# Hybrid SSD and gated-MLP block: a later place for one broadcast load, four small products and the splits of the turned copies

## The chip, the cores and the metric

The kernel runs on one core of a Trainium2 chip. The metric is device microseconds of one execution, the median of the timed runs. Before the change that is 978.47 us, the median of three runs (978.17, 978.47 and 980.12).

## The reference

One layer works on 256 latent tokens and 256 context tokens of width 2048. Cut to what matters here:

```python
zx = hx @ w_in                      # hx: normalised, modulated latents; 2048 wide in, z, u, v, m wide out
vn = rmsnorm(v) ; sg = w_s @ vn + b_s
y_b = rmsnorm(u * sg * silu(z_mlp)) * g_mlp     # the MLP half
y_a = rmsnorm(y_ssd * silu(z_ssd)) * g_ssd      # the SSD half
out = rmsnorm(concat(y_a, y_b) @ w_out) * g_post
x   = x + gate * out                # gate = silu(c) @ w_ada[:, 4096:] + b_ada[4096:]
```

All inputs are float32. A product with float32 weights is made of three TensorE products: each operand is split into a rounded part (hi) and the rest (lo), and hi*hi, hi*lo and lo*hi are summed. So each weight costs a cast on ScalarE (hi) and a subtraction on VectorE (lo) before TensorE can use it.

## The kernel before

**Stages.** The first 425 us make the modulation and the first projections and run the SSD scan. Then come the *latents*: sixteen blocks of 512 output columns, in the order v (blocks 0 to 3), u (4 to 7), m (8 to 11) and z (12 to 15). A block is 96 matmuls of 128x512: 16 slices of the inner dimension, two halves of the tokens, three products each. After the blocks come two output projections (`oproj`) and the finish.

**The weights' stream.** Weights come in 1 MB pieces on the queue of SyncE into four buffers. Half a piece at a time, ScalarE makes `hi_w` (L87) and VectorE `lo_w` (L88), each into one of four buffers; a half is worth 12 matmuls. The code asks for the split of a half three halves ahead of its use.

**What follows a block.** After a block of kind m or z, `lat_z` (L1123) takes its two PSUM tiles: ScalarE makes silu (`sz`), VectorE multiplies it into `vt` or `y`, ScalarE squares it for the norm. Then `lat_t` (L1057) turns the 512 columns: VectorE transposes 32x32 squares into a tile `T`, and sixteen DMAs of 32 KB, issued by GpSimd, put the squares in their places in a tile `Z` (the small transfers). Then `lat_split` (L1070), four times for a group: ScalarE makes the hi part of a turned slice times its norm weight (`hhi` or `yah`), VectorE the lo part (`hlo` or `yal`). They are operands of the output projections, a hundred microseconds and more later.

**The gate.** In blocks 1 to 8 VectorE sums the sixteen parts of the gate (`gate_tile`, L1011; its scratch tile is `junk`). `gate_bcast` (L1016), three units after block 9, makes from it a tile `G` of gate times g_post, the *output scale*, which only the finish uses. It loads g_post into G, broadcast to 128 partitions (1 MB written, queue of GpSimd), brings the gate into rows (a matmul `psgt`, then `gh`, `gl`), and then four times (`expand`, `spread`) VectorE makes a tile `gd`, TensorE spreads it over the partitions (`pg`, one matmul of 48x512) and VectorE multiplies the result into a quarter of G. There is one buffer for `gd`.

**What sets the order.** `later(dt, fn)` puts a function in a queue at a due time, in units that are meant as microseconds; `pump(1.3)` after every sixth matmul runs what is due. A block is 16 pumps, or 20.8 units. This gives the order in which the program is written down. From block 1 on, that order is not the one that runs: a planner goes through the program with its own costs of the instructions, and gives each engine in turn, among the instructions whose inputs and buffers are ready at that moment of its own clock, the one that stands first in the program. Within an engine, the chip then keeps the order so found, and an instruction that has to wait holds back all behind it.

Of the kernel before, what the change touches and what calls it, by code (L numbers as in the profile page):

```python
# [15 lines left out]
P = 128  # L16
# [31 lines left out]
def tile_hybrid_ssd_mlp(  # L48
# [19 lines left out]
    nc = tc.nc  # L68
    ORDER = _tile_order()

    def mkpool(**kw):
        return tc.tile_pool(reuse_waits="tile", **kw)
# [72 lines left out]
    def bc(ap, axis, n):  # L145
        u = ap.unsqueeze(axis)
        shp = list(u.shape)
        shp[axis] = n
        return u.to_broadcast(shp)
# [22 lines left out]
    def spt(shape, name):  # L172
        return sps.tile(shape, F32, tag="s", name=name)
# [390 lines left out]
    def half(u):  # L564
        if pos[1]:
            split_to(u + 4)
        else:
            later(0.1, lambda: split_hi(u + 3))
            later(1.4, lambda: split_lo(u + 3))
        return halves.pop(u)  # L570
# [6 lines left out]
    def later(dt, fn):  # L577
        queue.append((now[0] + dt, seq[0], fn))
        seq[0] += 1

    def pump(dt=0.0, flush=False):
        now[0] += dt
        while True:
            due = [q for q in queue if flush or q[0] <= now[0]]
            if not due:
                return
            q = min(due)
            queue.remove(q)
            q[2]()
# [409 lines left out]
    def open_lat():  # L999
        cvs.close()  # L1000
        L_["big"] = ctx.enter_context(mkpool(name="big", bufs=2, side="right"))
        L_["lt2"] = lt.enter_context(mkpool(name="lt2", bufs=2))
        gsp = gs.enter_context(mkpool(name="gsp", bufs=1))
        L_["vt"] = L_["big"].tile([P, 2, D], F32, tag="b16", name="vt")
        L_["cb2"] = gsp.tile([P, D], F32, name="cb2")
        L_["junk2"] = gsp.tile([P, D], BF16, name="junk2")
        nc.gpsimd.dma_start(L_["cb2"], crow.partition_broadcast(P))
        nc.scalar.activation(L_["cb2"], L_["cb2"], AF.Silu)


    def gate_tile(j):  # L1011
        raw = load_raw(wada[2 * KT + j], f"gate{j}")
        nc.vector.scalar_tensor_tensor(L_["junk2"], raw, 1.0, L_["cb2"], op0=ALU.mult, op1=ALU.mult,  # L1013
                                       accum_out=gate[:, j : j + 1])

    def gate_bcast():  # L1016
        gs.close()
        gp = ctx.enter_context(mkpool(name="gp", bufs=1, side="right"))
        G = gp.tile([P, D], F32, name="G")
        L_["G"] = G  # L1020
        nc.gpsimd.dma_start(G, gpost.partition_broadcast(P))
        nc.vector.tensor_tensor(gate[:, 0:16], gate[:, 0:16], pc[:, C_BADA + 32 : C_BADA + 48], op=ALU.add)
        nc.vector.tensor_copy(gate[:, 32:48], gate[:, 0:16])


        gh = gp.tile([48, P], F32R, name="gh")
        gl = gp.tile([48, P], F32R, name="gl")
        g1 = gp.tile([48, P], F32R, name="g1")
        gd = gp.tile([48, 4, P], F32R, name="gd")
        gk = gp.tile([48, KT], F32, name="gk")  # L1030
        nc.scalar.copy(g1, ones[0:48])
        nc.vector.tensor_tensor(gk, ident[0:48, 0:16], ident[0:48, 32:48], op=ALU.add)

        def rows():
            ps = spt([48, P], "psgt")
            nc.tensor.matmul(ps, lhsT=gate, rhs=ident, start=True, stop=True)
            nc.scalar.copy(gh, ps)
            nc.vector.tensor_tensor(gl, ps, gh.bitcast(F32), op=ALU.subtract)
            nc.vector.tensor_copy(gh[32:48], gl[32:48].bitcast(F32))

        def expand(j):
            nc.vector.tensor_tensor(gd, bc(gh.bitcast(F32), 1, 4), bc(gk[:, 4 * j : 4 * j + 4], 2, P), op=ALU.mult)

        def spread(j):
            p = spt([P, 512], f"pg{j}")
            nc.tensor.matmul(p, lhsT=g1, rhs=gd, start=True, stop=True)
            gb = G[:, j * 512 : (j + 1) * 512]
            nc.vector.tensor_tensor(gb, p, gb, op=ALU.mult)
            if j < 3:
                expand(j + 1)  # L1050

        later(2, rows)
        later(4, lambda: expand(0))
        for j in range(4):
            later(7 + 3 * j, lambda j=j: spread(j))

    def lat_t(kind, j4):  # L1057
        src = L_["vt"] if kind == 2 else y
# [11 lines left out]
    def lat_split(kind, j):  # L1070
        src = L_["Z"][:, :, j % 4]
        if kind == 2:
            gcol, hi, lo = C_GMLP, hhi[j][:, 0:256], hlo[j][:, 0:256]
        else:
            gcol, hi, lo = C_GSSD, L_["yah"][:, j, :], L_["yal"][:, j, :]
        hi, lo = (t.rearrange("p (t c) -> p t c", t=2) for t in (hi, lo))
        gc = pc[:, gcol + j : gcol + j + 1]
        nc.scalar.mul(hi, src, gc)
        nc.vector.scalar_tensor_tensor(lo, src, gc, hi.bitcast(F32), op0=ALU.mult, op1=ALU.subtract)
# [10 lines left out]
    def lat_vn(j4):  # L1090
        cols = slice(j4 * 512, (j4 + 1) * 512)
        gw = L_["lt2"].tile([P, 1024], F32, tag="gw", name=f"gw{j4}")
        gvb, ws = gw[:, 0:512], gw[:, 512:1024].rearrange("p (g q) -> p g q", g=4)
        nc.gpsimd.dma_start(gvb, gv[:, cols].partition_broadcast(P))
        nc.gpsimd.dma_start(ws, wsp[:, 4 * j4 : 4 * j4 + 4, :])
        for tk in range(2):
            vb = L_["vt"][:, tk, cols]
            nc.vector.scalar_tensor_tensor(vb, vb, rr[:, 0, tk : tk + 1], gvb, op0=ALU.mult, op1=ALU.mult)
        L_["ws"] = ws

    def lat_sg(j4):
        ws = L_["ws"]
        L_["sg"] = []
        for tk in range(2):
            p = spt([P, 512], f"psg{j4}{tk}")
            for gi in range(4):
                g = 4 * j4 + gi
                nc.tensor.matmul(p[:, gi * P : (gi + 1) * P], lhsT=ws[:, gi, :],
                                 rhs=L_["vt"][:, tk, g * P : (g + 1) * P], start=True, stop=True)
            L_["sg"].append(p)  # L1110
# [29 lines left out]
    for blk in range(16):  # L1140
        kind, j4 = divmod(blk, 4)
        if blk == 0:

            pa = [acp.tile([P, 512], F32, tag="acc", name="pa00"), spt([P, 512], "pa01")]
        elif blk % 2 == 0:
            pa = [acp.tile([P, 512], F32, tag="acc", name=f"pa{blk}{tk}") for tk in range(2)]
        else:
            pa = [spt([P, 512], f"pa{blk}{tk}") for tk in range(2)]
        if kind == 1:
            later(3 if j4 == 0 else 0, lambda j4=j4: lat_vn(j4))  # L1150
            later(10, lambda j4=j4: lat_sg(j4))
        for u in range(8):
            whi, wlo = half(base + blk * 8 + u)
            for kk in range(2):
                k = 2 * u + kk
                w = slice(kk * 512, (kk + 1) * 512)
                for tk in range(2):
                    t = slice(256 + tk * P, 256 + (tk + 1) * P)
                    nc.tensor.matmul(pa[tk], lhsT=hhi[k][:, t], rhs=whi[:, w], start=k == 0, stop=False)  # L1159
                    nc.tensor.matmul(pa[tk], lhsT=hhi[k][:, t], rhs=wlo[:, w], start=False, stop=False)  # L1160
                    nc.tensor.matmul(pa[tk], lhsT=hlo[k][:, t], rhs=whi[:, w], start=False, stop=k == KT - 1)  # L1161
                pump(1.3)
            if blk == 0 and u == 7:
                pump(flush=True)
                man.close()
                pos[1] = max(halves) + 1
                open_lat()
            if 1 <= blk < 9 and u % 4 == 1:
                gate_tile((blk - 1) * 2 + u // 4)
        if kind == 0:  # L1170
            later(0, lambda j4=j4, pa=pa: lat_v(j4, pa))
        elif kind == 1:
            later(0, lambda j4=j4, pa=pa: lat_u(j4, pa))
        else:
            later(0, lambda kind=kind, j4=j4, pa=pa: lat_z(kind, j4, pa))
            later(1.5, lambda kind=kind, j4=j4: lat_t(kind, j4))
            for jj in range(4):
                later(17 + jj, lambda kind=kind, j=4 * j4 + jj: lat_split(kind, j))
        if blk == 9:
            later(3, gate_bcast)  # L1180

# [4 lines left out]
    G, yah, yal = L_["G"], L_["yah"], L_["yal"]  # L1186
# [197 lines left out]
```

## Time and profile before

| | |
|---|---|
| median of the timed runs | 978.47 us (978.17 to 980.12) |
| the profiled execution's own time | 981.04 us |
| its span in the profile | 979.3 us |
| granted TensorE clock, mean | 0.996 |
| TensorE busy | 968.3 us (99%) |
| VectorE, ScalarE, GpSimd busy | 665.1, 496.0, 186.6 us |
| first matmul of block 9, 10, 11, 12 | 636.64, 658.40, 687.75, 709.64 us |

The profiled execution took 981.04 us, 1.74 us more than the span of its instructions and 2.57 us more than the median. Times inside it are microseconds from the start of the span. PE is TensorE, DVE is VectorE, ACT is ScalarE, POOL is GpSimd and SP is SyncE. A matmul of 128x512 is shown with about 0.39 us, but its successor starts 0.227 us later: the busy time of PE overlaps with itself, and time lost on PE is read from the distance of the starts or from the waits.

### The profile page before, as it was taken

How to read it: one execution, taken by the hardware profiler on the slowest of the kernel's cores; microseconds unless marked ns; L12 is line 12 of the kernel's file. 1: busy time of each engine (PE TensorE's matmuls, PEld its weight loads, DVE VectorE, ACT ScalarE, POOL GpSimd, SP SyncE). 2: the span in 40 equal slices, each digit the busy share in tenths (PEclk: the TensorE clock that was granted, in tenths of full speed). 3: DMA queues.
4: the chain of work that ended last, by engine and by line, in shares of the span. 5: the costliest groups of instructions: out<-in, count | busy, mean ns of one | idle time of the engine just before them, and what ended most of it. 6: DMA issues, size and time to landing. Idle time of an engine off the chain costs nothing.

```text
span 979.3 us, 13757 instructions
## 1 busy us (share of the span) xinstructions
PE 968.3 (99%) x5242; PEld 781.8 (80%) x5242; DVE 665.1 (68%) x1075; ACT 496.0 (51%) x757; POOL 186.6 (19%) x290
## 2 busy tenths in 40 slices
PE   9999999999999999999999999999999999999997
PEld 4688888787887878787888888886888888888885
DVE  6888798778876665755766776666666665445636
ACT  4344458666565454645444443444566564345522
POOL 0000002541462122124000000043333451000000
PEclk9999999999999999999999999999999999999999
DMA  9999953332333423146787778785666666556722
GB/s 366 417 415 415 371 217 130 110 133 86 129 106 132 151 86 130 47 169 221 300 301 281 266 255 309 269 302 168 213 209 199 235 219 207 201 186 241 271 89 86
DMA packets 37090, 211.45 MB, mean 216 GB/s; under 512 B 6417, under 2 KB 6673, under 8 KB 14369
## 3 DMA queue, kind: packets, MB, share of 16 engines
q1 hardware_dynamic: 30240, 192.91, 53.2%
q0 software_dynamic: 6208, 16.85, 5.2%
q8 instruction: 41, 0.67, 0.3%
q10 hardware_dynamic: 576, 0.82, 0.2%
q14 instruction: 25, 0.20, 0.1%
HBM read 204.20 MB, written 2.16 MB: 211 GB/s over the span
## 4 chain that ended last, share of the span: by engine, by line
PE 78%; DMA 11%; DVE 6%; issue 3%; ACT 2%; POOL 0%; SPq 0%; DVEq 0%; ACTq 0%; POOLq 0%
PE psx L141 9%; PE psx L143 9%; PE psx L142 9%; PE pa L1159 7%; PE pa L1160 7%; PE pa L1161 7%; DMA gate<-in_wada_dram 5%; PE pm L1202 3%; PE pm L1201 3%; PE pm L1200 3%; DMA ada<-in_wada_dram 3%; DVE lo_w L88 3%; PE pq L1202 2%; PE pq L1201 2%; PE pq L1200 2%
## 5 line engine op out<-in xcount | busy, mean ns | idle before, releaser
L88 DVE TENSOR_TENSOR lo_w<-w,hi_w 128x1024 fp32r<-128x1024 f32 x173 | 209.7, 1221 | 127.9 <-ACT hi_w L87 127.9
L87 ACT CAST hi_w<-w 128x1024 fp32r<-128x1024 f32 x173 | 181.9, 1053 | 210.5 <-PE pa L1161 146.3
L1159 PE MATMUL pa<-hi_w,hhi 128*128 128x512 f32 x512 | 201.7, 394 | 0.0
L1160 PE MATMUL pa<-lo_w,hhi 128*128 128x512 f32 x512 | 200.2, 391 | 1.3 <-DVE lo_w L88 1.3
L1161 PE MATMUL pa<-hi_w,hlo 128*128 128x512 f32 x512 | 199.9, 390 | 0.0
L141 PE MATMUL psx<-hhi,hi_w 128*128 128x512 f32 (+1 forms) x400 | 153.4, 383 | 0.0
L143 PE MATMUL psx<-hhi,lo_w 128*128 128x512 f32 (+1 forms) x400 | 145.9, 365 | 0.0
L142 PE MATMUL psx<-hlo,hi_w 128*128 128x512 f32 (+1 forms) x400 | 145.7, 364 | 0.0
L1160 PEld LDWEIGHTS pa<-lo_w,hhi 128*128 128x128 f32 x512 | 96.4, 188 | 21.8 <-DVE lo_w L88 2.0
L1159 PEld LDWEIGHTS pa<-hi_w,hhi 128*128 128x128 f32 x512 | 96.5, 189 | 21.4 <-issue 1.6
L1161 PEld LDWEIGHTS pa<-hi_w,hlo 128*128 128x128 f32 x512 | 96.5, 189 | 20.3
L623 DVE SCALAR_TENSOR_TENSOR xbc<-psx,pc,xbc 128x248 f32<-128x248 f32 (+1 forms) x204 | 83.6, 471 | 34.5 <-ACT xbc L607 33.5
L548 DVE TENSOR_TENSOR lo_w<-w,hi_w 128x1024 fp32r<-128x1024 f32 x61 | 77.1, 1271 | 23.7 <-ACT hi_w L542 23.6
L1067 POOL DMA_DIRECT2D Z<-T x128 | 73.9, 584 | 97.4 <-DVE T L1062 28.8
L141 PEld LDWEIGHTS psx<-hhi,hi_w 128*128 128x128 f32 x400 | 75.5, 189 | 13.3 <-issue 2.9
L143 PEld LDWEIGHTS psx<-hhi,lo_w 128*128 128x128 f32 x400 | 75.4, 189 | 12.5
L142 PEld LDWEIGHTS psx<-hlo,hi_w 128*128 128x128 f32 x400 | 75.6, 189 | 12.2 <-issue 1.7
L542 ACT CAST hi_w<-w 128x1024 fp32r<-128x1024 f32 x61 | 63.5, 1044 | 26.0 <-PE psx L142 12.9
L1013 DVE SCALAR_TENSOR_TENSOR junk<-gate,cb 128x2048 bf16<-128x2048 f32 x16 | 36.7, 2291 | 27.9 <-DMA gate<-in_wada_dram 27.9
L1200 PE MATMUL pm<-hi_w,hhi 128*128 128x512 f32 x128 | 49.8, 389 | 0.0
L1201 PE MATMUL pm<-lo_w,hhi 128*128 128x512 f32 x128 | 49.8, 389 | 0.0
L1202 PE MATMUL pm<-hi_w,hlo 128*128 128x512 f32 x128 | 49.8, 389 | 0.0
(270 smaller groups left out, 1398.9 us busy)
## 6 DMA issues: line engine op xcount, KB each, us to landing
w<-in_wlat_dram SPq DMA_DIRECT2D x64, 1024.0 KB, 4.9
w<-in_wout_dram SPq DMA_DIRECT2D x32, 1024.0 KB, 4.8
w<-in_wxbc_dram SPq DMA_DIRECT2D x25, 1024.0 KB, 4.8
ada<-in_wada_dram SPq DMA_DIRECT2D x24, 1024.0 KB, 13.9
gate<-in_wada_dram SPq DMA_DIRECT2D x16, 1024.0 KB, 5.9
ada<-in_wada_dram SPq DMA_DIRECT2D x16, 512.0 KB, 12.3
R<-acs POOLq DMA_DIRECT2D x8, 1024.0 KB, 5.7
wst<-in_wst_dram SPq DMA_DIRECT2D x15, 480.0 KB, 12.9
```

Source lines behind the costliest of these rows:

```text
L87: nc.scalar.copy(hi, raw)
L88: nc.vector.tensor_tensor(lo, raw, hi.bitcast(F32), op=ALU.subtract)
L141: nc.tensor.matmul(ps, lhsT=whi, rhs=hhi[k][:, s], start=start, stop=False)
L142: nc.tensor.matmul(ps, lhsT=whi, rhs=hlo[k][:, s], start=False, stop=False)
L143: nc.tensor.matmul(ps, lhsT=wlo, rhs=hhi[k][:, s], start=False, stop=stop)
L623: nc.vector.scalar_tensor_tensor(ao, zi, cw[:, k : k + 1], ao, op0=ALU.mult, op1=ALU.add)
L1159: nc.tensor.matmul(pa[tk], lhsT=hhi[k][:, t], rhs=whi[:, w], start=k == 0, stop=False)
L1160: nc.tensor.matmul(pa[tk], lhsT=hhi[k][:, t], rhs=wlo[:, w], start=False, stop=False)
L1161: nc.tensor.matmul(pa[tk], lhsT=hlo[k][:, t], rhs=whi[:, w], start=False, stop=k == KT - 1)
L1200: nc.tensor.matmul(p, lhsT=yh[:, t], rhs=whi[:, w], start=j == 0, stop=False)
L1201: nc.tensor.matmul(p, lhsT=yh[:, t], rhs=wlo[:, w], start=False, stop=False)
L1202: nc.tensor.matmul(p, lhsT=yl[:, t], rhs=whi[:, w], start=False, stop=hf == 0 and j == 15)
```

## The change

Three due times change. The load of g_post into G leaves the start of `gate_bcast` and gets a due time six units behind it. The four `spread` steps go from 7, 10, 13, 16 to 17, 20, 23, 26 units behind it. The `lat_split` steps (eight groups of four) go from 17, 18, 19, 20 to 19, 20, 21, 22 units behind the end of their block. No instruction is added or taken away.

```diff
     def gate_bcast():
         ...
         L_["G"] = G
-        nc.gpsimd.dma_start(G, gpost.partition_broadcast(P))
         nc.vector.tensor_tensor(gate[:, 0:16], gate[:, 0:16], pc[:, C_BADA + 32 : C_BADA + 48], op=ALU.add)
         ...
         later(2, rows)
         later(4, lambda: expand(0))
+        later(6, lambda: nc.gpsimd.dma_start(G, gpost.partition_broadcast(P)))
         for j in range(4):
-            later(7 + 3 * j, lambda j=j: spread(j))
+            later(17 + 3 * j, lambda j=j: spread(j))
     ...
             for jj in range(4):
-                later(17 + jj, lambda kind=kind, j=4 * j4 + jj: lat_split(kind, j))
+                later(19 + jj, lambda kind=kind, j=4 * j4 + jj: lat_split(kind, j))
```

## Prediction, made before the changed kernel was run

> **What bounds the kernel now.** TensorE: it is busy for 99% of the span, so only time that TensorE loses can be won. I looked for where it loses any, first in the table of stretches, cut at the first matmuls of blocks 9 to 12 (columns: stretch, its length, busy time of each engine, granted clock, DMA share, GB/s).
>
> ```profile
> PE 968.3 (99%) x5242; PEld 781.8 (80%) x5242; DVE 665.1 (68%) x1075; ACT 496.0 (51%) x757; POOL 186.6 (19%) x290
> ```
> ```profile
> 636.64:658.40 21.76, 21.76 (x97) 18.02 (x96) 15.75 (x18) 10.55 (x15) 8.31 (x15) 1.00 0.85 296
> 658.40:687.75 29.35, 27.23 (x104) 19.39 (x102) 19.01 (x28) 14.02 (x24) 10.75 (x19) 0.94 0.61 199
> 709.64:731.40 21.76, 21.76 (x97) 18.02 (x96) 13.91 (x20) 13.56 (x21) 9.24 (x16) 1.00 0.65 218
> ```
>
> A clean block is 21.76 us, or 0.2267 us a matmul. Block 10 takes 29.35: 7.59 us more, and it is the block that holds the gate's products. The waits and the matmuls around them say where these go (timeline rows: start, duration, engine, line, tiles, in brackets the idle time before and what ended it).
>
> ```profile
> PE pa L1160 <- DVE lo_w L88: 1.3, 2, 0.8
> PE pg L1046 <- DVE gd L1042: 0.9, 1, 0.9
> ACT hhi L1078 <- DMA Z<-T: 7.5, 1, 7.5
> ```
> ```profile
> 671.98 0.50 PE L1160 MATMUL pa<-lo_w,hhi 128*128 128x512 f32 x1 [0.51 <-DVE lo_w L88]
> 673.02 0.40 PE L1161 MATMUL pa<-hi_w,hlo 128*128 128x512 f32 x1
> 674.27 0.49 PE L1046 MATMUL pg<-gd,g 48*128 48x512 f32 x1 [0.85 <-DVE gd L1042]
> 678.90 0.39 PE L1161 MATMUL pa<-hi_w,hlo 128*128 128x512 f32 x1
> 679.21 0.50 PE L1046 MATMUL pg<-gd,g 48*128 48x512 f32 x1
> 679.64 0.51 PE L1159 MATMUL pa<-hi_w,hhi 128*128 128x512 f32 x1
> ```
> ```profile
> 664.73:668.15 3.42, 2.96 (x12) 1.58 (x10) 2.66 (x5) 3.42 (x8) 0.00 (x0) 1.00 0.01 2
> 671.56:674.97 3.41, 2.14 (x7) 1.32 (x8) 3.34 (x6) 1.80 (x2) 3.41 (x7) 1.00 0.73 187
> 674.97:678.39 3.42, 3.42 (x9) 2.65 (x9) 2.72 (x4) 0.95 (x1) 2.76 (x5) 0.50 1.03 356
> ```
>
> The reader is to see four losses. Two waits for `lo_w`, 1.3 us together, and about 1.7 with the slow restart of the pipeline. One wait of 0.9 for the first `gd`. A stretch of 3.4 us at half clock, right behind a stretch of equal length in which PE was idle for 3.41-2.14 = 1.27 us, or 37%; it costs half of 3.41, 1.7 us. And the gate's own products: from 678.90 to the matmul after 679.64 would be two steps without `pg` (0.45 us); it is 0.31+0.43+0.34 = 1.08 (the last step is estimated like the first), so each `pg` costs 0.63, four 2.5 us.
>
> **Why lo_w was late** is in the rows of ACT, DVE and POOL.
>
> ```profile
> 655.88 1.05 ACT L87 CAST hi_w<-w 128x1024 fp32r<-128x1024 f32 x1 [1.67 <-PE pa L1161]
> 664.49 1.71 ACT L1078 ACTIVATE hhi<-Z,pc 128x256 fp32r<-128x256 f32 x4 [7.55 <-DMA Z<-T]
> 666.10 1.04 ACT L87 CAST hi_w<-w 128x1024 fp32r<-128x1024 f32 x1
> 670.74 2.32 DVE L88 TENSOR_TENSOR lo_w<-w,hi_w 128x1024 fp32r<-128x1024 f32 x2
> 673.53 0.68 DVE L1042 TENSOR_TENSOR gd<-gh,gk 48x512 fp32r<-48x512 f32 x1
> ```
> ```profile
> 454.11 0.54 POOL L1094 DMA_DIRECT2D gw<-in_gv_dram  x1
> L1098 DVE SCALAR_TENSOR_TENSOR vt<-vt,rr,gw x8: 746/750/752, 526.4 to 564.1; 128x512 f32<-128x512 f32 x8
> 640.76 0.54 POOL L1021 DMA_DIRECT2D G<-in_gpost_dram  x1 [82.36 <-DVE junk L1013]
> 647.10 4.65 POOL L1067 DMA_DIRECT2D Z<-T  x8 [5.81 <-DVE T L1062]
> 659.32 1.16 POOL L1067 DMA_DIRECT2D Z<-T  x2 [0.54 <-DMA Z<-T]
> ```
>
> The four `hhi` of the first group stand in ACT's order ahead of the next `hi_w`, and their small transfers land only at 664.4. ACT stands still for 7.55 us, and the weights' splits behind it come late. The load of G was issued at 640.76, ahead of the sixteen small transfers on the same queue.
>
> **The change, part by part.**
>
> *The load of G.* In the program it already stands behind the small transfers of two groups: `gate_bcast` is due three units after block 9, at about 662, and `lat_t` of block 9 at 1.5. It ran at 640.76 all the same, when the last `junk` freed its memory and POOL had nothing else. A load of the u blocks shows the same: it ran at 454.11, its data are used at 526.4. The planner takes what is ready; `T` of the first group was not (POOL waited 5.81 us for it). Six units later in the program make G no later ready, and nothing is ready in its stead. So I take its place and its time as unchanged, 0 us; cover is not needed.
>
> *The splits.* They too run by readiness: by the code the first two `hhi` of the group stand ahead of the `hi_w` of 655.88 (due at pump 14, that one before pump 15), and they ran behind it, all four at a stretch. Two units later the first two still stand ahead of the `hi_w` of 666.10 and take the same place; the last two may fall behind it. The second late `lo_w`, which ends at 673.06 less one lo of 1.2, that is about 671.9, has the same work ahead of it either way, and it alone sets when TensorE resumes (671.98). Bounds: 0 to -0.4 us; I take 0, since the later wait absorbs what the first gives.
>
> *The spreads.* TensorE is never idle in the plan, so there the place in the program does decide. The first `pg` moves from pump 9 of block 10 to pump 1 of block 11, the others to pumps 3, 5 and 7. What this removes: the wait of 0.9 for `gd`, which is ready since 674.2. With it the idle share of the stretch up to 674.97 falls from 37% to some 12%, as in the stretch at 664.73 (2.96 busy of 3.42, full clock behind it): the half-clock stretch goes, 1.7 us. The four products themselves cost 2.5 us here or there.
>
> *What is late next.* Without products and half clock, the 47 matmuls after 671.98 take 47 x 0.2267 + 0.1 = 10.8 us, so block 11 begins at 682.75 and not at 687.75. The second group's turned copies do not move with it.
>
> ```profile
> 679.00 2.88 POOL L1067 DMA_DIRECT2D Z<-T  x5 [1.27 <-DMA Z<-T]
> DMA to landing us min/median/max: 1.8/4.2/8.4
> 685.66 1.71 ACT L1078 ACTIVATE hhi<-Z,pc 128x256 fp32r<-128x256 f32 x4
> 687.27 0.58 ACT L1131 ACTIVATE sz<-pa 128x512 f32<-128x512 f32 x1
> 676.41 0.68 DVE L1048 TENSOR_TENSOR G<-pg,G 128x512 f32<-128x512 f32 x1
> 677.01 0.67 DVE L1042 TENSOR_TENSOR gd<-gh,gk 48x512 fp32r<-48x512 f32 x1
> 690.25 1.28 DVE L1133 TENSOR_TENSOR vt<-vt,sz 128x512 f32<-128x512 f32 x2
> ```
>
> The last of the sixteen is issued at 681.3 and needs at least 1.8: it lands at 683.1 or later. ACT wants it 687.75-685.66 = 2.1 us before block 11, now at 680.7, and waits 2.6 us. Behind it on ACT are `sz` and `hi_w`, and on DVE `hlo`, a `lo_w`, the two `vt`, and then the product into G and the second `gd`, for which the second `pg` waits on TensorE. From the first `hhi` to the end of the second `vt` it was 691.53-685.66 = 5.87 us, with one product into G (0.6) in between; then come G and `gd` (1.3): 683.3 + 5.3 + 1.3 = 689.9. TensorE comes to the second `pg` at 682.75 + 18 x 0.2267 + 0.63 = 687.5. That is a wait of 2.4 us at most, 2.0 if the planner puts `pg` two matmuls further back for it; if it puts G and `gd` ahead of `lo_w` and one `vt` (1.2 + 0.6), 0.4. Nothing in the trace shows this order, so I take the middle, 1.2. Cover for the weights is ample: the delayed `lo_w` is wanted only six pumps into block 11, at 692.
>
> *Sum.* -0.9 (wait for the first `gd`) + 1.2 (new wait for the second) = +0.3, and -1.7 where the half clock was. Against the profiled execution's own 981.04 this is 979.6. That execution is 2.57 us above the median, and of the three runs one, 980.12, stands 1.65 above the next: about the price of a half-clock stretch. I choose to read the median as a run without it, and add to it only the +0.3: **978.8 us**.
>
> By the Trainium skill (TensorE: Matmul & The Clock Gate, Part 1: The HAM clock gate) the activity window is 3413 ns long and free-running, so that the same program meets it in another phase each time. The stretch of half clock from 674.97 to 678.39 agrees in length, and it would make the -1.7 us a matter of the single run, as I chose. The same section has the clock fall after an idle window; in this trace it fell after one with 37% idle, so the measurement decides.
>
> **Rivals.**
>
> *The load of G does go behind the first small transfers.* For it speaks only that the program says so. DMA moves some 377 GB/s at best here, so 1 MB less ahead gives 2.8 us: ACT resumes at 661.7, both waits for `lo_w` (1.7) go as well as the 0.9. Block 11 then begins at 680.8, the second group lands 2.8 earlier too, and the new wait is 0 to 1.2: 978.5-2.6+0.6 = 976.5 us.
>
> ```profile
> 644.00:648.00 4.00, 4.00 (x20) 3.30 (x19) 4.00 (x6) 3.45 (x7) 0.90 (x2) 1.00 0.93 377
> ```
>
> *VectorE keeps up and the second `pg` waits for nothing.* For it: in block 10 three of four `pg` waited for nothing, with two pumps between them as after. Against: there no `vt` stood between. 978.5-0.9 = 977.6 us, down to 975.9 if the median had the half clock.
>
> *Slower: the second `pg` waits 2.0 to 2.4 us in one piece and the clock falls.* Place: 18 matmuls into block 11. From the point where PE's idle share of a 3.41 us stretch passes a limit between 13% and 37%, it costs 1.7 more: 978.5-0.9+2.2+1.7 = 981.5 us. Against: a wait of 2 us is often cut in two by the stretches' border. A sentence beside it: by the skill's idle window this would cost 979.8, since no window is wholly idle.
>
> **How the numbers follow.** The forecast (new wait between 0.4 and 2.0, 977.7 to 979.8) has 0.50, the load that moves 0.12, VectorE that keeps up 0.22, the fall of the clock 0.16. A measurement of this kernel tells about 0.2%, 2 us, from no change, so faster is under 976.5 and slower over 980.4. Faster: half of 0.12, a third of 0.22 and a little of the first, 0.19. Slower: most of 0.16 and a little of the first, 0.17. Same: 0.64. The range of 976.0 to 980.8 leaves out the lower end of two rivals and most of the slower one's upper part, some 2 in 10.
>
> **What would show it.** Right: the load of G still first on POOL, with the first small transfers behind it; ACT's wait of some 7.5 us for the first group as before, TensorE's two waits for `lo_w` too; no wait of the first `pg`, then in block 11; block 10 about 5 us shorter, block 11 longer by 2.5 us and by a wait for `gd`; ACT with a wait of about 2.6 us for the second group. Wrong: G's load issued behind 647, or ACT's wait under 5 us; then the planner does follow the due times. A time under 976 would mean that, over 981 that the new wait brought the clock down.

## The result and the profile after

The changed kernel takes **985.3 us** (median of 6 runs, 984.24 to 988.06) against 979.19 for the kernel before in the same batch (6 runs, 978.17 to 980.12). The ratio is 1.0066, with a 95% interval of 1.0051 to 1.0080: slower by 0.66%, 6.1 us. The prediction was 978.8 us, with a range of 976.0 to 980.8, so the time lies outside it, and on the side of the rival to which I gave a chance of 0.16.

The profiled execution of the changed kernel has a span of 986.3 us (its time is 988.06); before it was 979.3. Both profiled executions stand above their medians, by 1.9 us (981.04, before) and 2.8 us, so each is on the long side and the two are compared with each other. First the busy times by engine, from the page:

```profile
PE 969.6 (98%) x5242; PEld 782.2 (79%) x5242; DVE 664.3 (67%) x1075; ACT 495.4 (50%) x757; POOL 186.2 (19%) x290
```

TensorE does the same 5242 matmuls in nearly the same busy time (969.6 against 968.3 us), and the span is 7.0 us longer. So the loss is idle time of TensorE, and it is found with the table of stretches, cut at the first matmuls of blocks 9, 10, 11 and 12 (columns as in the prediction: stretch, length, busy time of PE, PEld, DVE, ACT, POOL, granted clock, DMA share, GB/s):

```profile
637.71:659.47 21.76, 21.76 (x98) 18.02 (x96) 15.65 (x18) 10.45 (x15) 8.00 (x14) 1.00 0.86 306
659.47:684.32 24.85, 23.19 (x99) 17.95 (x98) 14.60 (x19) 11.96 (x19) 11.01 (x20) 1.00 0.63 208
684.32:716.66 32.34, 26.82 (x101) 20.05 (x100) 18.25 (x24) 13.57 (x22) 9.20 (x16) 0.89 0.47 152
```

Of the kernel before, the one row of this table that the prediction did not show, block 11:

```profile
687.75:709.64 21.89, 21.89 (x97) 18.13 (x97) 13.67 (x17) 11.60 (x18) 9.22 (x16) 1.00 0.59 195
```

Block 10 became 4.50 us shorter (29.35 to 24.85), as was meant. Block 11 became 10.45 us longer (21.89 to 32.34): TensorE is busy for only 26.82 of it, and the granted clock is 0.89. The two together are 57.19 against 51.24, 5.95 us more. Of the 7.0 us of span, another 0.93 lie in block 8 (22.69 against 21.76), where this one execution shows a wait of 0.6 for a `lo_w`, ahead of all that the change touches.

The waits of TensorE and ACT on the changed kernel (engine, tile, line, who it waited for: total us, number, longest):

```profile
PE pg L1045 <- DVE gd L1041: 5.5, 1, 5.5
PE pa L1160 <- DVE lo_w L88: 1.7, 2, 1.1
PE pa L1159 <- ACT hi_w L87: 0.4, 1, 0.4
ACT hhi L1078 <- DMA Z<-T: 14.7, 2, 8.4
```

Of the 1.7 for `lo_w`, 0.6 is the wait in block 8; block 10 has 1.1 and the 0.4 for a `hi_w`. The wait of 0.9 us for the first `gd` is gone. In its place stands one wait of 5.5 us for a `gd`, and ACT waits twice for turned copies that arrive late, where before it waited once. The rows around the second wait, in order of time (timeline: start, duration, engine, line, operation, tiles; in brackets the idle time before it and what ended it):

```profile
642.47 0.54 POOL L1053 DMA_DIRECT2D G<-in_gpost_dram  x1 [84.00 <-DVE junk L1013]
648.81 4.64 POOL L1067 DMA_DIRECT2D Z<-T  x8 [5.81 <-PE pa L1161]
...
680.67 2.88 POOL L1067 DMA_DIRECT2D Z<-T  x5 [1.43 <-DMA Z<-T]
...
689.14 1.31 ACT L1078 ACTIVATE hhi<-Z,pc 128x256 fp32r<-128x256 f32 x3 [6.28 <-DMA Z<-T]
689.51 0.39 PE L1161 MATMUL pa<-hi_w,hlo 128*128 128x512 f32 x1
...
692.36 1.22 DVE L88 TENSOR_TENSOR lo_w<-w,hi_w 128x1024 fp32r<-128x1024 f32 x1
693.49 0.69 DVE L1133 TENSOR_TENSOR vt<-vt,sz 128x512 f32<-128x512 f32 x1
694.09 0.68 DVE L1047 TENSOR_TENSOR G<-pg,G 128x512 f32<-128x512 f32 x1
694.70 0.67 DVE L1041 TENSOR_TENSOR gd<-gh,gk 48x512 fp32r<-48x512 f32 x1
695.42 0.79 PE L1045 MATMUL pg<-gd,g 48*128 48x512 f32 x1 [5.52 <-DVE gd L1041]
696.14 0.79 PE L1159 MATMUL pa<-hi_w,hhi 128*128 128x512 f32 x1
```

Read backwards: the second `pg` starts at 695.42, when `gd` is done. Before `gd` on VectorE come the product into G, a `vt`, a `lo_w`, two `hlo`, another `vt` and the first two `hlo`; this chain began with the first `hhi` on ACT at 689.14, and that waited 6.28 us for the second group's small transfers, the last of which POOL had started before 683.55. The load of G still stands first on POOL, ahead of all small transfers.

The idle time cost the clock as well. The four stretches around the wait:

```profile
686.95:690.36 3.41, 2.95 (x13) 2.08 (x12) 0.68 (x2) 1.22 (x4) 0.00 (x0) 1.00 0.02 10
690.36:693.77 3.41, 0.00 (x0) 0.00 (x0) 3.02 (x6) 3.41 (x8) 0.00 (x0) 1.00 0.00 0
693.77:697.19 3.42, 1.77 (x4) 1.14 (x5) 3.42 (x6) 1.16 (x3) 0.04 (x1) 0.50 0.72 247
697.19:700.60 3.41, 3.41 (x10) 2.64 (x9) 2.92 (x4) 1.04 (x1) 3.41 (x7) 0.50 0.34 103
```

One stretch is wholly idle, and then the clock is at half for two. TensorE had work from 695.42 to 700.60 of it; half of these 5.18 us is 2.6 lost. So the 5.95 us of blocks 10 and 11 come together in this way: -0.9 (the wait for the first `gd`) -1.7 (the half clock of before) +5.5 (the new wait) +2.6 (the new half clock) +0.2 (waits for the first group's late weights, 1.1+0.4 in place of 1.3) = 5.7.

**Why the second group came so late** is in the weights' stream. The table of stretches again, two microseconds at a time (the two last columns are DMA), and the timeline of SP's queue with the load of one weight piece (1 MB), under the `lo_w` that it waited for. First the kernel after:

```profile
679.50:681.50 2.00, 2.00 (x10) 1.65 (x10) 1.23 (x1) 0.64 (x1) 0.83 (x2) 1.00 1.06 371
681.50:683.50 2.00, 2.00 (x11) 1.65 (x10) 0.61 (x1) 1.05 (x1) 2.00 (x4) 1.00 0.96 295
683.50:685.50 2.00, 2.00 (x11) 1.61 (x9) 0.61 (x1) 0.00 (x0) 0.05 (x1) 1.00 0.98 365
685.50:687.50 2.00, 2.00 (x9) 1.26 (x8) 0.00 (x0) 0.00 (x0) 0.00 (x0) 1.00 0.39 141
```
```profile
680.17 1.23 DVE L88 TENSOR_TENSOR lo_w<-w,hi_w 128x1024 fp32r<-128x1024 f32 x1 [1.00 <-ACT hi_w L87]
681.42 0.33 SPq L81 DMA_DIRECT2D w<-in_wlat_dram  x1
```

The same two views of the kernel before:

```profile
679.80:681.80 2.00, 2.00 (x9) 1.64 (x10) 1.23 (x2) 0.46 (x1) 2.00 (x4) 1.00 0.88 298
681.80:683.80 2.00, 2.00 (x8) 1.23 (x7) 1.38 (x2) 0.59 (x1) 0.09 (x1) 1.00 0.17 34
683.80:685.80 2.00, 2.00 (x10) 1.66 (x9) 1.04 (x3) 1.09 (x2) 0.00 (x0) 1.00 0.52 123
```
```profile
682.42 1.23 DVE L88 TENSOR_TENSOR lo_w<-w,hi_w 128x1024 fp32r<-128x1024 f32 x1 [1.39 <-ACT hi_w L87]
683.68 0.33 SPq L81 DMA_DIRECT2D w<-in_wlat_dram  x1
```

Before, the last small transfer of the second group was issued at 681.30 and its end came at 683.33: 2.0 us, in a DMA that was at 17%. The next piece of weights was asked for after that, at 683.68. In both kernels the load starts when a `lo_w` ends and frees a buffer (681.40, before 683.65), and the `hi_w` ahead of that `lo_w` had waited for TensorE (1.66 us, before 2.85). After, TensorE is ahead (block 11 begins 3.4 us earlier), has used up an earlier piece sooner, and so the next one is asked for at 681.42, in the middle of the last five small transfers. The last of them was issued at 682.97 and landed at 688.99: 6.0 us, with DMA at 96 to 98% until 685.5. From 684.1 to the landing the profile shows no work on VectorE or GpSimd, so neither of them holds the transfers up. The issue itself is also 1.7 us later than before. On VectorE the second group's `vt` and `T` stand behind the first group's `hlo`, and ACT came out of its wait for the first group at 666.38, before at 664.49. This delay is older than what the change moves: the last `junk` of the gate already starts at 639.62, before at 637.90.

In short: without the products in block 10 TensorE runs ahead, its pace brings a load of 1 MB among the second group's last small transfers, these land 4 us later, and ACT, VectorE and in the end TensorE stand still for them. The experiments test this.

### The profile page after: what moved, and what is told of

Its sections match the earlier page's. It is cut to its first block, busy times and chain, and to the rows that moved or that the text cites. A ratio compares the mean times of both kernels' runs of the same rounds, so it can differ in the third digit from the quotient of the medians.

```text
span 986.3 us, 13757 instructions
## 1 busy us (share of the span) xinstructions
PE 969.6 (98%) x5242; PEld 782.2 (79%) x5242; DVE 664.3 (67%) x1075; ACT 495.4 (50%) x757; POOL 186.2 (19%) x290
## 4 chain that ended last, share of the span: by engine, by line
PE 78%; DMA 11%; DVE 5%; issue 2%; ACT 2%; POOL 1%; SPq 0%; DVEq 0%; ACTq 0%; POOLq 0%
PE psx L141 9%; PE psx L143 9%; PE psx L142 9%; PE pa L1159 8%; PE pa L1160 8%; PE pa L1161 8%; DMA gate<-in_wada_dram 4%; PE pm L1201 3%; PE pm L1200 3%; PE pm L1202 3%; DMA ada<-in_wada_dram 3%; DMA Z<-T 2%; PE pq L1200 2%; PE pq L1201 2%; PE pq L1202 2%
```

## The experiments

The theories that the expectations name: the spreads alone make the loss (against: the later load or the later splits do, or all together); the wait is made by the weight piece that comes earlier; the spreads in block 11 cost nothing of themselves if the first group is in time (against: a product at a block's border is dear anywhere). The runs of the kernel before that each ratio goes by have medians of 978.74 to 978.80 (979.19 for the row "after"); a ratio need not be the quotient of two medians to the last digit. Summary first (stretches of each profiled execution; "ACT waits" are those for turned copies of the first and second group, where no other number is said):

| kernel | median us | ratio, 95% | block 10 | block 11 | ACT waits us | wait at `pg` |
|---|---|---|---|---|---|---|
| before | 979.19 | | 29.35 | 21.89 | 7.5 | 0.9 |
| after | 985.3 | 1.0066 (1.0051-1.0080) | 24.85 | 32.34 | 8.4, 6.3 | 5.5 |
| spreads alone | 985.27 | 1.0067 (1.0050-1.0084) | 22.71 | 31.37 | 11.6 in two | 4.9 |
| all but the spreads | 978.40 | 0.9991 (0.9980-1.0001) | 25.95 | 21.90 | 8.8 in two | 0.9 |
| spreads still later | 985.76 | 1.0067 (1.0047-1.0086) | 23.26 | 24.40 | 6.8, 5.1, five more | 0 |
| piece held too long | 988.87 | 1.0096 (1.0081-1.0112) | | | 11.9 in four | 1.7 |
| piece held | 980.78 | 1.0027 (1.0011-1.0043) | 24.62 | 28.44 | 8.1, 3.2 | 2.4 |
| after, G really behind | 985.11 | 1.0069 (1.0052-1.0086) | 22.34 | 30.03 | 5.6, 4.8 | 4.0 |
| before, G really behind | 977.24 | 0.9989 (0.9980-0.9999) | 24.82 | 21.89 | 3.7, 0.4 | 0 |
| G behind, spreads still later | 981.54 | 1.0027 (0.9994-1.0061) | 22.34 | 24.37 | 0, 0 | 0 |
| before, gate's parts earlier | 976.63 | 0.9973 (0.9962-0.9984) | 24.82 | 21.89 | 0 | 0 |
| after, gate's parts earlier | 976.73 | 0.9983 (0.9974-0.9993) | 22.33 | 24.38 | 0 | 0 |

### The spreads alone, and all but the spreads

In the kernel before one line is changed:

```diff
-            later(7 + 3 * j, lambda j=j: spread(j))
+            later(17 + 3 * j, lambda j=j: spread(j))
```

And in the kernel after the same line is put back:

```diff
-            later(17 + 3 * j, lambda j=j: spread(j))
+            later(7 + 3 * j, lambda j=j: spread(j))
```

> The kernel before with the four spreads alone moved (17, 20, 23, 26); load and splits as before. Theory A (the second spread runs into ScalarE's wait for the second group's turned copies, and that wait is long because a weight load now comes 2 us ahead of their last transfers): the splits add nothing, about 984 to 986 us, block 11 some 31 to 33 us long. Theory B (the splits behind the silu push the second half of T, and with it the small transfers, 1.5 us back, and that is what costs): about 979 to 981 us, the wait for the second gd under 3 us.

> The changed kernel with the four spreads back at 7, 10, 13, 16; load and splits as changed. Theory A: as the kernel before, 978 to 980.5 us, the first pg waiting about 0.9 us or a little more in block 10. Theory B: some of the loss stays, 982 us or more.

Measured 985.27 and 978.40 us. Stretches and wait of the kernel with the spreads alone:

```profile
658.47:681.18 22.71, 22.63 (x99) 18.02 (x98) 14.52 (x19) 12.04 (x19) 9.21 (x16) 1.00 0.61 207
681.18:712.55 31.37, 26.47 (x101) 19.81 (x100) 18.35 (x24) 13.56 (x22) 9.23 (x16) 0.89 0.49 158
```
```profile
PE pg L1046 <- DVE gd L1042: 4.9, 1, 4.9
```

The same wait and the same clock of 0.89 without the other two edits. And the other two edits without the spreads change nothing that can be told: the interval holds 1. The whole loss is the spreads, and the due times of the load and of the splits do nothing measurable, as the prediction had it for both.

### The spreads still later

```diff
-            later(17 + 3 * j, lambda j=j: spread(j))
+            later(27 + 3 * j, lambda j=j: spread(j))
```

> The changed kernel with the spreads ten units further back (27, 30, 33, 36): they fall on pumps 8 to 14 of block 11, when ScalarE has come out of its wait. Theory A: the wait for the second gd is gone, block 10 keeps its 24.9 us, block 11 takes about 25 to 27 us (four products and up to 2 us of wait for a late lo_w): 977 to 980 us. Rival C (block 11 bears no products in any place, since its VectorE is full): 983 us or more.

Measured 985.76 us, the time of rival C and not of theory A. The part about the place held, against rival C: blocks 10 and 11 take 47.66 us, 3.6 less than before, and no `pg` waits. The stretches of blocks 10, 11, 13 and 14, and ACT's waits:

```profile
658.40:681.66 23.26, 22.95 (x99) 17.95 (x98) 14.60 (x19) 11.96 (x19) 9.21 (x16) 1.00 0.60 205
681.66:706.06 24.40, 24.40 (x101) 18.44 (x100) 15.79 (x21) 10.75 (x17) 9.22 (x16) 1.00 0.66 222
727.82:751.74 23.92, 22.37 (x97) 17.91 (x96) 13.61 (x16) 13.19 (x19) 10.22 (x18) 1.00 0.58 197
751.74:775.26 23.52, 22.38 (x97) 17.86 (x96) 13.51 (x16) 11.80 (x18) 9.23 (x16) 1.00 0.61 203
```
```profile
ACT hhi L1078 <- DMA Z<-T: 24.7, 4, 6.8
ACT yah L1078 <- DMA Z<-T: 17.9, 3, 6.8
```

But now ACT waits for the turned copies of seven groups in a row, 5.1 to 6.9 us each. Blocks 13 and 14, clean in the kernel before, take 23.92 and 23.52; the first products of the output then wait 1.7 and 1.5 us more, and the clock falls at 806. While ACT waits, no `hi_w` is made, then several are made at once, and the pieces of weights are asked for in bunches: four between 713.3 and 724.9, then none until 738.2. Each bunch comes in the next group's small transfers. This is read from the order in one trace. So the late product into the second `pg` was not the only place where the loss could show: the late copies are what lasts, and the `pg` was only the first to meet them.

### One piece of weights held back

In the changed kernel, the piece that came at 681.42 is held back by a copy of one column from a turned tile into the piece's buffer, which the load then overwrites. The first version reads another group's tile than the second's:

```diff
-            raws[pos[0]] = load_raw(stream[pos[0]], f"w{pos[0]}")
+            if pos[0] == 73:
+                raws[73] = wp["raw"].tile([P, 2048], F32, tag="raw", name="w73")
+                nc.gpsimd.tensor_copy(raws[73][:, 0:1], L_["Z"][:, 0, 0, 0:1])
+                nc.sync.dma_start(raws[73], stream[73])
+            else:
+                raws[pos[0]] = load_raw(stream[pos[0]], f"w{pos[0]}")
```

> The changed kernel, with the one weight load that was issued at 681.4, ahead of the last five small transfers of the second group, held until those have landed (GpSimd copies one column of the turned tile into the load's buffer first, so the load waits for that copy; the column is then overwritten). Theory A: the last of the second group lands about 684 and not 689, ScalarE's second wait falls from 6.3 us to about 1 to 2, the wait for the second gd from 5.5 to 1 to 2, no half clock: 978.5 to 981 us. Theory B (the transfers are slow of themselves, having started 1.5 us later): landing at 687 or later, 984 us or more.

Measured 988.87 us. The tile that it read was the third group's by then, and the piece came at 699.51 instead of behind 682. The second group's copies did land 2.3 us after the last issue (681.91 after 679.62), and the wait at `pg` fell to 1.7; but TensorE then waited 4.7 us for a `hi_w` out of the held piece, block 12 took 24.94, and the clock was at half for 6.83 us from 711.26. So the time of this kernel says nothing on the question, but its second group does: no piece is asked for between 674.70 and 686.53, the last transfer lands 2.3 us after its issue, ACT waits 2.5 us and TensorE 1.7.

```profile
PE pg L1050 <- DVE gd L1046: 1.7, 1, 1.7
```

The second version plans the hold earlier, so that it reads the second group's tile, and sets the third group's small transfers behind it (the first line stands in `load_to`, the last around the transfers of `lat_t`):

```diff
+        n = 74 if n == 73 else n
...
+                L_["hold"] = nc.gpsimd.tensor_copy(raws[73][:, 0:1], L_["Z"][:, 0, 0, 0:1])
...
+                with (tc.issue_after(L_["hold"].ins) if (kind, j4) == (2, 2) else ExitStack()):
```

> The changed kernel with the weight piece that was loaded at 681.4 held until the second group's sixteen transfers have landed (GpSimd copies one column of Z into the piece's buffer first; the load overwrites it). In the run before this one the copy read the third group's tile, so the piece came 18 us late; now it reads the second's. Theory A (that load is what makes the last five transfers late): they land 2 to 3 us after the last issue and not 6, the wait for the second gd is 1 to 2.5 us and not 5.5, no half clock, 979 to 982 us. Theory B: the wait stays over 4 us, 984 us or more.

Measured 980.78 us, that is 4.5 us less than the changed kernel (3.8 by the two ratios, which go by runs of the kernel before in the same batch). Timeline rows, the wait, and the stretch of block 11:

```profile
684.01 0.33 SPq L535 DMA_DIRECT2D w<-in_wlat_dram  x1
685.87 1.31 ACT L1085 ACTIVATE hhi<-Z,pc 128x256 fp32r<-128x256 f32 x3 [3.18 <-DMA Z<-T]
```
```profile
PE pg L1051 <- DVE gd L1047: 2.4, 1, 2.4
```
```profile
684.16:712.60 28.44, 26.01 (x101) 19.48 (x100) 18.21 (x24) 13.57 (x22) 9.20 (x16) 0.94 0.57 186
```

The piece is asked for 2.6 us later (684.01 in place of 681.42). The last small transfer, issued at 682.46, then lands at 685.72, 3.3 us after and not 6.0. ACT's wait falls from 6.28 to 3.18, TensorE's from 5.5 to 2.4, and one half-clock stretch is left of two. The last issue moved by 0.5 us only. So most of the late landing is a collision with this one load of the weights' stream. What the profiled execution has left is a wait of 2.4 and one half-clock stretch, where the expectation had none; but it is the longest of the six (984.00), and three of them show a granted clock of 0.999, where it shows 0.997, so the half clock is not in every run. The hold also did less than was expected of it: the column is written by the first four of the sixteen transfers, the copy ran at 683.04, right behind the last issue, and the piece was asked for before the last transfer had landed. It moved the piece from ahead of the last issue to behind it.

The other kernels agree with this reading. Where the piece is asked for ahead of the last issue, the second group's last transfer lands late: 6.0 us after its issue in the changed kernel (piece 1.6 ahead), 5.8 with the spreads alone (1.2), 5.1 with the spreads still later (1.3), and 4.9 in the changed kernel with G behind, which follows (1.1). Where it is asked for behind the issue, the landing takes 2.0 (before), 2.2 (all but the spreads), 3.3 (piece held) and 3.7 (before, G behind). The lateness matters because the issue is late as well: in the four kernels named first it stands 1.3 to 1.7 us before the start of block 11, in the kernel before 6.4.

### The load of G truly behind the small transfers

The due time did not move the load. This edit does, by an order between the two (the last small transfer of the first group first):

```diff
+        with tc.issue_after(L_["zl", 2, 0].ins):
             nc.gpsimd.dma_start(G, gpost.partition_broadcast(P))
```

It was put into the changed kernel, into the kernel before, and into the changed kernel together with the spreads at 27.

> The changed kernel with the load of G in truth behind the first group's sixteen transfers on GpSimd's queue (an order edge from the last of them). If the load ahead of them costs them what 1 MB takes at 377 GB/s: the first group lands 2.8 us earlier, ScalarE's first wait falls from 8.4 to about 5.5 us, block 10 loses its waits for lo_w (23 us or less and not 24.9). The second group then still meets the spreads in block 11: 978 to 985 us in all, according to whether the second group lands by the end of block 10.

> The kernel before with nothing but the load of G behind the first group's transfers (order edge); spreads and splits at their old due times. Same reason as for the run with both: ScalarE's first wait 7.5 -> about 5, the waits for lo_w in block 10 gone, the first pg with a wait under 0.5: 975 to 977.5 us. If the load's place did not matter: 978 to 980.

> The changed kernel with the load of G behind the first group's transfers and the spreads at 27, 30, 33, 36. With the spreads at 27 alone ScalarE waited 5 to 7 us for the turned copies in each of seven groups, because the weight loads that had been held up by one such wait ran in a bunch into the next group's transfers. If the first wait starts that row, a shorter first wait (5 us) still starts it: 980 to 986 us. If it ends it: 974 to 977 us.

In the changed kernel: 985.11 us, no gain that can be told. G is issued at 658.46, behind all sixteen. Block 10 is clean, 22.34 us, without the waits for `lo_w`; the second group's copies are still late (ACT waits 4.75 us) and `pg` waits 4.0. In the kernel before: 977.24 us, at the edge of what can be told. Its block 10 has no wait of TensorE at all, and ACT waits little (stretch, then wait):

```profile
658.49:683.31 24.82, 24.82 (x104) 18.43 (x102) 18.92 (x28) 13.76 (x23) 9.21 (x16) 1.00 0.77 255
```
```profile
ACT hhi L1080 <- DMA Z<-T: 4.1, 2, 3.7
```

With the spreads at 27 as well, the ten runs fall into two clusters, five at 976.79 to 977.47 and five at 985.61 to 987.97; the median of 981.54 stands for neither. The profiled execution is of the lower cluster, and in it TensorE waits for nothing in these blocks; ACT waits once, 1.1 us, for the third group (the stretches of blocks 10 and 11):

```profile
658.74:681.08 22.34, 22.34 (x99) 18.11 (x98) 14.90 (x20) 12.75 (x21) 9.22 (x16) 1.00 0.75 259
681.08:705.45 24.37, 24.37 (x101) 18.45 (x100) 18.35 (x25) 12.86 (x20) 9.21 (x16) 1.00 0.63 215
```

The upper cluster is at the time of the kernel with seven late groups. Whether it is the same row of waits, started or not by how the first group lands, is not shown: no execution of that cluster has a profile. The granted clock of its runs is 0.994 to 0.997, in the lower cluster 0.998 to 0.999, and in the runs of the kernel with seven late groups 0.997 to 0.999, so the two need not be alike.

### The first group in time

If the first group's lateness starts all this, then an earlier start of the gate's work must help both kernels. The sixteen parts of the gate's weights (`gate_tile`), two a block in blocks 1 to 8, are put earlier, so that POOL is free and `junk` done long before the first turn:

```diff
+    GATES = {1: (1, 4, 6), 2: (1, 4, 6), 3: (1, 4, 6), 4: (1, 5), 5: (1, 5), 6: (1, 5), 7: (1,)}
+    gseq = list(range(16))
...
-            if 1 <= blk < 9 and u % 4 == 1:
-                gate_tile((blk - 1) * 2 + u // 4)
+            if u in GATES.get(blk, ()):
+                gate_tile(gseq.pop(0))
```

> The kernel before with the sixteen gate parts summed earlier (three a block in blocks 1 to 3, two in 4 to 6, the last in 7, where it was two a block in 1 to 8), everything else as before. The last gate part then holds back neither the first group's vt and T (4.2 us of wait on VectorE) nor the weight pieces in block 9, and G's memory is free before the first group's transfers. Theory A (the first group's lateness starts all of it): ScalarE's first wait falls from 7.5 us to under 2, block 10 takes 24.5 to 26 us and not 29.4, no later wait: 974 to 976.5 us, unless the extra megabytes in blocks 1 to 3 cost there. If the lateness comes from something else: 978 to 980.

> The changed kernel with the same earlier gate parts. Theory A: with the first group in time there is no late second group for the spreads in block 11 to run into: wait for the second gd under 1.5 us, 974.5 to 977.5 us, about as the kernel before with them, so the change's loss of 6 us is gone. Rival C (spreads at the border of two blocks are bad of themselves, since VectorE is full there): 5 to 6 us more than the kernel before with earlier gate parts, 980 to 984 us.

On the kernel before 976.63 us (10 runs, 976.49 to 977.17), a little above the 974 to 976.5 expected, and faster than the kernel before by 0.27% (0.16 to 0.38): this version beats both kernels. On the changed kernel 976.73 us. The blocks 10 and 11 of the first, then of the second:

```profile
658.55:683.37 24.82, 24.82 (x104) 18.43 (x102) 18.78 (x28) 13.03 (x21) 9.18 (x16) 1.00 0.62 211
683.37:705.26 21.89, 21.89 (x98) 18.12 (x97) 13.67 (x17) 11.60 (x18) 9.19 (x16) 1.00 0.59 195
```
```profile
660.59:682.92 22.33, 22.33 (x99) 18.11 (x98) 14.87 (x20) 12.74 (x21) 9.20 (x16) 1.00 0.64 213
682.92:707.30 24.38, 24.38 (x102) 18.44 (x100) 17.78 (x24) 12.14 (x19) 9.20 (x16) 1.00 0.58 195
```

Both make 46.71 us, TensorE busy throughout and at full clock. The products cost 2.5 us in the one block or in the other. With the first group in time, moving them does nothing, neither gain nor loss; so the border of blocks 10 and 11 is not a bad place of itself, and the change's loss needs the late first group. The collision itself is still there: in both, and in the profiled execution with G behind and the spreads later, a piece is asked for 1.1 to 1.4 us ahead of the second group's last issue, which lands 4.4 to 4.7 us later. But that issue now stands 6.9 to 9.6 us before block 11, and nothing waits for it. One limit: this edit moves G's load too (to 605.8), so it doesn't tell that load from the gate's parts; the kernel before with G alone behind, at 977.24, suggests that about half of the gain is G's 1 MB out of the first group's way (0.11% of 0.27%). In the changed kernel G alone behind did not help (985.11), so there it takes more than that.

## Why the prediction was wrong, point by point

- **The load of G: right.** It ran first on POOL at 642.47, ahead of the first small transfer at 648.81, and without the spreads the rest of the change measured 0.9991.
- **The splits: right in effect.** The last two of the first group did fall behind a `hi_w` (ACT had two `hhi` at 666.38 and two at 669.71). TensorE's waits for the first group's weights were 1.5 us and not 1.3, outside the 0 to -0.4 that I gave; but the kernel with all but the spreads has the same splits, shows none of these waits in block 10, and measures as before.
- **The spreads, in block 10: right.** The first `pg` went to block 11 (685.77) and waited for nothing, the wait of 0.9 and the half clock behind it are gone, and block 10 is 4.5 us shorter, where 5.0 was forecast.
- **What is late next: wrong, and this is the step that failed.** It names the right chain. From the first `hhi` to the end of the second `gd` it was 6.2 us (689.14 to 695.37), where I had 5.3+1.3 = 6.6; and TensorE came to the second `pg` after 21 matmuls of the block at 689.74, where I had 687.5. The term that failed is the landing of the second group: "it lands at 683.1 or later", and I went on with 683.3. It landed at 688.99. I had taken the shortest landing of all (1.8 us) on top of an issue time of the kernel before, with the words "or later" in the text and no upper end in the sum, although the same row had 4.2 as the median and 8.4 as the longest. Of the 5.7 us, 1.7 are the later issue, and 4.0 the longer landing, 6.0 in place of 2.0. With a short landing the rest of the chain comes out as forecast: in the kernel with the piece held too long it was 2.3, and there ACT waited 2.5 us (forecast 2.6) and the second `pg` 1.7 (forecast 0.4 to 2.4).
- **What I left out:** I let TensorE be 5 us ahead in block 10 and asked only which operand would be late for it. I did not ask what else its pace releases. It frees the weights' buffers, so the next 1 MB is asked for 2.3 us earlier (681.42, before 683.68), inside the small transfers that I had put down as unmoved. The run with that one piece moved behind the last issue shows it: with it 3.8 to 4.5 of the 6.1 us go.
- **The sum.** The wait for the second `gd` was 1.2 by the forecast and at most 2.4; it was 5.5. The half clock was to go by 1.7 and not to return; it came back at 2.6. The choice to read the median as a run without a half clock fits later runs of the kernel before: those near their median show a granted clock of 0.998 to 0.999, the profiled execution 0.996. One slip: 0.4 to 2.0 of new wait gives 978.0 to 979.6 by the forecast's own terms, not 977.7 to 979.8.
- **The rivals.** The load of G behind the small transfers was priced at 976.5 with a new wait of 0 to 1.2; done by an order, it measured 985.11 with a wait of 4.0, so this rival had the same term wrong. Its 377 GB/s is not the best in the trace either: the page of the kernel before has slices of 417. "Slower" had the right mechanism, a wait at the second `pg` in one piece and the clock that falls, at a chance of 0.16 and with 2.2+1.7 us as its price; its size was off by the same landing. The argument against it, that a wait of 2 us is often cut by a stretch's border, fell with the wait's size: one of 2 us can't fill a stretch of 3.41 us, one of 5.5 us can, and here it did. Near the forecast's size it was a matter of the single run: with the piece held, a wait of 2.4 us has a half-clock stretch in the profiled execution, and three of the six runs show a clock of 0.999. That the Trainium skill's idle window would spare the clock ("no window is wholly idle") fell with it. By the Trainium skill (TensorE: Matmul & The Clock Gate, Part 1: The HAM clock gate) the clock falls after an idle window, and here it did, behind a stretch with 0.00 us of matmuls. In the kernel before a stretch with 37% idle was enough, so there the measurement decides against that rule as the only one.
- **The range** was made of waits between 0 and 2.4 us. Had the landing been carried with its own row (1.8 to 8.4), the copies would have come up to 681.3+8.4 = 689.7, `gd` 6.6 later at 696.3, and the wait would have run up to 8.8 us; the range's upper end would have stood past 985.

What the Trainium skill says of queues would have been a warning: each DMA engine goes round its queues a packet at a time (DMA: Bandwidth & Descriptors, Queues, rings and completion order), so a 1 MB load asked for in the middle of small transfers on another queue shares the engines with them and doesn't stand behind them. The traces agree in direction (2.0 us at a DMA share of 0.17, 6.0 us at 0.96 to 0.98); no run here looks at single packets.

**What stays open.** Why the kernel before, whose first group is as late (7.5 us), does not fall into the row of waits: by its trace block 10 takes 7.6 us more than a clean one and the stream has that time to catch up, but no run takes this away and leaves all else. Why this execution of the changed kernel is 1.7 us late at the last `junk`, of which 0.9 is block 8. Whether the upper cluster of the kernel with G behind and the spreads at 27 is that row of waits. And why the changed kernel's last small transfers land only at 688.99, while DMA is already at 0.39 between 685.5 and 687.5.

## What to carry to other kernels

When an edit lets the bounding engine run ahead, its pace sets more than when operands are wanted: it frees buffers, and so starts the next loads of the stream earlier; work out when those loads will start and which short transfers will be in flight then. A transfer's landing must go into the sum with its whole spread (here 1.8 to 8.4 us for one kind of transfer), not with its least. And a due time in a plan that takes what is ready acts only on the engine that never lacks work: to move a load truly, make it wait for what it should follow.

## What was not expected of the hardware

- The same small transfer (the second group's last of sixteen on POOL's queue) lands 2.0 to 3.7 us after its issue when the next 1 MB load is asked for behind it (four kernels), 2.3 us when none is near, and 4.4 to 6.0 us when that load is asked for 1.1 to 1.6 us ahead of it (seven kernels).
- Half clock comes in whole stretches: 3.41 us once, behind a stretch with TensorE idle for 37% of it (kernel before) or busy for 0.98 of 3.41 us (piece held, 688.90 to 692.31), 6.83 us behind a wholly idle stretch (after, and the kernel with the piece held too long).
- Late small transfers can go on being late: seven groups in a row, with waits of 5.1 to 6.9 us each, 138 us from the first to the last (663.72 to 801.67). And the times of one kernel fall into two clusters 9 us apart, with five runs in each; what parts them is open.
